# Decay rows of the mLSTM spread by one 128-row float32r product, and a 128-row low product for the last down k-tile

## The chip, the cores and the metric

One NeuronCore of one Trainium2 chip runs the whole kernel. Times are device microseconds (us) of that core, from runs of the same program; a profile is one execution seen by the hardware profiler. TensorE (PE) does the matrix products, ScalarE (ACT) and VectorE (DVE) do elementwise work, GpSimd (POOL) small side jobs, SyncE (SP) issues the transfers.

## The reference

Two layers over 256 tokens of width 1024, all in float32. Only the parts that the change touches are written out:

```python
def hybrid_layer(h, p_i, ...):
    h = h + 0.5 * swiglu(rmsnorm(h, ffn1_norm), w_gate, w_up, w_down)   # (silu(x Wg) * (x Wu)) Wd, inner width 2752
    u = rmsnorm(h, mix_norm); z = u @ w_in
    hm = mlstm_chunkwise(mq, mk, mv, ig, lf)        # 4 heads of 256
    ha = swa_gqa_sinks(aq, ak, av, a_sinks)
    h = h + (sigmoid(g_m) * (hm @ w_branch_m) + sigmoid(g_a) * (ha @ w_branch_a)) @ w_out
    h = h + 0.5 * swiglu(rmsnorm(h, ffn2_norm), ...)
    return h + sigmoid(rmsnorm(h, ple_norm) @ ple_gate_w) * (p_i @ ple_proj_w)

# inside mlstm_chunkwise: per head, weights exp(a[s] - M[t]) between tokens s <= t,
# a = input gate - running sum of log forget gates, M = running maximum of a
```

## The kernel before

Each float32 product is carried by float32r products of parts: x = xh + xl and w = wh + wl, where the high part is rounded to float32r and the low part is the rest; `mm3` issues xh·wh, xh·wl and xl·wh into one PSUM accumulation. Weights stream from memory in raw tiles of 1 MB (two buffers). Each is cut into parts of 128 x 1024; ScalarE rounds a part into `wh`, VectorE subtracts to get `wl` (`splitting`), and eight split parts fit on the chip. TensorE, ScalarE, VectorE and SyncE issue in the order in which the Python code runs; `tick()` advances background chains (generators that yield where the next stage has to wait) by an estimated clock, `Clock`, so a chain with one stage more is issued later. GpSimd's order is left to the framework.

A layer runs ffn1, mix, ffn2 and the per-layer embedding (ple). Two places matter.

The down product of an ffn (`down_run`; tile `dn`; 4 in the program) has 2752 = 21·128 + 64 inner rows, so 22 k-tiles. k-tiles 0 to 17 go to all four outputs (token tile t, half n) in turn. The last four go output by output: 3 + 3 + 3 + 2 products for one output, then the next. For the last k-tile the hidden layer's 64 rows are stored twice in one tile of 128 rows, the high part on rows 0 to 63 and the low part on 64 to 127, against the weight rows, also stored twice. One 128-row product gives xh·wh + xl·wh; the product xh·wl takes 64 rows only (`p=low`, `lo[low]`).

The decays of the mLSTM (`decays`, tile `wt`; 4 heads in each of 2 layers) need the row -M[t] of a head on all 128 partitions. The four rows lie in `nM`, 4 x 384 in float32. A float32 product of 4 rows with one column of the identity, broadcast over 128 columns, spreads one of them; two bf16 products add the causal mask. These groups stand between the products of branch A (tile `ya`), in the chain `scans`, after five small transposes of the gates (`tp<-ident,gates`) and their copy `gcols`.

The norm that follows an ffn (`norm`: sums on ACT, `ms` on DVE, the power `r` on POOL, `xn` on DVE, transposes on TensorE) begins for token tile 0 while TensorE works on the outputs of token tile 1.

Of the kernel before, what the change touches and what calls it, by code (L numbers as in the profile page):

```python
# [11 lines left out]
F32 = mybir.dt.float32  # L12
# [21 lines left out]
RAW = 2                 # raw weight tiles  # L34
RING = 8                # split weight parts on chip
STORE, HASTE = 4, 3     # parts split and not begun: enough of them, and what suffices in haste
AHEAD = (3.0, 2.0)      # how far the splitting engines' queues may be ahead of TensorE: until STORE is reached, then
ACTIVE = 5              # attention groups at work at a time
LATE = 4                # k-tiles of the hidden layer that come output by output
# [10 lines left out]
class Part:  # L50
    """k k-tiles of n weight columns, from column c0 of the raw tile: split into high and low when fed."""

    def __init__(self, c0, k, n):
        self.c0, self.k, self.n = c0, k, n
        self.hi = self.lo = self.ready = None
        self.fresh = True


class Clock:
    """An estimate (us) of when each engine is through with what it was given, from which the order of issue follows.  # L60
    The instructions of a stage take each other's results: an engine's first one starts after the others' so far, and
    VectorE's also after ScalarE's."""
# [43 lines left out]
    def load(self, ready, mb=1.0):  # L106
        """A transfer that may start at ready -> when it arrives."""
        latency, per = self.DMA
        self.dma = max(self.dma, ready, self.now) + mb * per
        return self.dma + latency  # L110


class Timed:
    """An engine whose instructions are charged to the clock."""
# [25 lines left out]
class XT:  # L140
    """The two parts of a transposed activation [nk * 128, T]: hi, lo(k, tok[, n]) is n of its k-tiles (one: 2-d).
    wait() moves the chains on that still have to write what is about to be read."""
# [20 lines left out]
class Trunk:  # L163
    """Every float32 product x @ w is carried as xh @ wh + xh @ wl + xl @ wh, where
    xh is x rounded to float32r and xl = x - xh, which float32r holds exactly.

    TensorE, ScalarE and VectorE issue in the order written here. The products with the weights are cut into steps
    of about 1.3 us; before each, tick() splits weights that come later and moves the chains in the background
    (norms, transposes, attention) on, so that what TensorE meets next has been ready for a while."""

# [24 lines left out]
    def tick(self):  # L195
        """Moves on the chains whose next stage is ready by TensorE's time, then feeds."""
        for chain in list(self.bg):
            if chain[1] <= self.clock.now:
                self.advance(chain)
        self.feed()  # L200
# [9 lines left out]
    def later(self, chain, ready=0.0):  # L210
        """A generator: it yields where what follows has to wait for what it issued."""
        self.bg.append([chain, max(self.clock.done(), ready)])
        return self.bg[-1]
# [13 lines left out]
    def defer(self, fn, *args):  # L227
        """fn(*args), once what it reads is ready; what it yields, if anything, are stages of a chain."""
        def chain():
            more = fn(*args)  # L230
            if more is not None:
                yield from more
        return self.later(chain())

# [13 lines left out]
    def consts(self):  # L248
# [9 lines left out]
        nc.vector.memset(self.ones, 1.0)  # L258

        def mask(out, base, step, channel):  # L260
            """0 where base + step * column + channel * row >= 0, else NEG."""
# [11 lines left out]
    def load(self, parts, *copies):  # L273
        """Registers a load, in the order of use: copies (raw -> destination, DRAM source) and what it is cut into."""
# [3 lines left out]
    def columns(self, src, p=None):  # L278
        """Registers src [128, k, n]."""
# [5 lines left out]
    def unit(self, w, c0, n=NB):  # L285
        """Registers columns c0..c0+n of w [1024, .]."""
# [7 lines left out]
    def halves(self, src):  # L294
        """Registers two units by halves of their k-tiles; src(u, h) is a list of (raw -> view, DRAM source)."""
# [11 lines left out]
    def prefetch(self, n=RAW, cut=False):  # L307
        """Issues loads until n raw tiles are under way (cut: each in two transfers)."""
# [12 lines left out]
    def feed(self, must=False):  # L321
        """Starts to split the next weight part if it is there and the queues are short enough, or if it must."""
# [20 lines left out]
        def chain():  # L343
            yield from self.splitting(hi, lo, raw[:, part.c0 : part.c0 + w])
# [12 lines left out]
    def need(self, part):  # L357
        """Has part split before a product with it is issued."""
# [20 lines left out]
    def project(self, units, xT, base, use, first=0, last=0):  # L379
        """x @ each unit; use(n, t, ps) takes unit n for token tile t. The first and the last parts are used for token  # L380
        tile 0 and then for token tile 1, the others for both at once."""
# [29 lines left out]
    def project_T(self, unit, xT, base):  # L411
        """(x @ unit)^T -> PSUM banks [features, 2 * T], two feature tiles in each."""
# [4 lines left out]
    def project_halves(self, units, xT, base, use):  # L417
        """The same for each unit; use(i, ps) takes the feature tiles i, i + 1. The first half of x's k-tiles goes to
        all units before the second does."""
# [36 lines left out]
    def transposes(self, src, n):  # L456
        """src [P, n*128] -> PSUM [P, n, 128]."""
# [28 lines left out]
    def first_gain(self, vec):  # L486
        """The same in PSUM: products with ones, which also have TensorE's clock up when the first rows arrive."""
# [12 lines left out]
    def power(self, out, x):  # L500
        """out = x ** -0.5"""
        self.nc.gpsimd.tensor_tensor(out, x, self.mhalf[:, : x.shape[-1]], op=ALU.pow)

    def norm(self, t, ss, g, xT):
        """A chain: the normed token tile, transposed and split into xT."""
# [15 lines left out]
    def first_norm(self, t, g, xT):  # L521
        """The norm of the input; the first weight part's split (entry) goes between its products and its copies."""
# [11 lines left out]
    def sink(self, scale, following):  # L534
        """(prepare, then): then(n, t, y) adds scale * y to half n of token tile t of the residual stream and goes on
        to the norm that follows: (gain vector, xT), or None after the last block."""
# [22 lines left out]
    def ffn(self, xT, wg, wu, wd, sink, first=6):  # L559
# [22 lines left out]
        def swiglu(pg, pu, k):  # L582
            """A chain: the transposed hidden layer from k-tile k on, from silu(gate) and banks [features, n * T]. Of the
            last rows, high and low lie one below the other in the first part's tile."""
# [23 lines left out]
        def last_features(c0):  # L608
            """The last features' gate and up columns side by side in one stationary tile."""
# [15 lines left out]
        for k0 in range(0, nk - 2, 2):  # L625
# [3 lines left out]
                          *[(lambda raw, p=p: raw[p, D:], wd[(nk - 1) * P :, :]) for p in (low, high)])  # L629

        def down_run():
# [3 lines left out]
            def tile_mm(t, n, k):  # L635
# [4 lines left out]
                else:  # L640
                    nc.tensor.matmul(acc[t, n], hT[0](k, tok), hi, start=False, stop=False)
                    nc.tensor.matmul(acc[t, n], hT[0](k, tok, p=low), lo[low], start=False, stop=True)
# [22 lines left out]
    def ple(self, l, xT, sink):  # L665
        """sigmoid(x) is (1 + tanh(x / 2)) / 2 here and in mix, as tanh shares a table with silu and with exp; the sink's
        scale takes the half in."""
# [42 lines left out]
    def mix(self, l, xT, sink):  # L710
        """ga, gm and the merged branches carry twice their values, which the sink's scale takes back."""
# [37 lines left out]
        def job_T(units, xT, base, use, before=None):  # L749
            """use(k, ps) takes the k-tiles k, k + 1 of the transposed product [features, 2 * T]."""  # L750
# [6 lines left out]
        def gate(c0):  # L757
            """tanh(gate / 2) by k-tiles, transposed."""
# [47 lines left out]
    def per_feature(self, l):  # L806
        """Per-partition columns: conv taps (k, tile), conv bias (tile), q and k gains (both halves)."""
# [60 lines left out]
class Mlstm:  # L868
    """Matrix memory in parallel form over two blocks of 128 tokens."""
# [7 lines left out]
    def prepare(self, w_in):  # L877
        """The loads for the gates."""
# [10 lines left out]
    def gate_weights(self):  # L889
        """The 8 gate columns as a stationary tile of 128: high i, f at columns 0, 32, low i, f at columns 64, 96."""  # L890
# [8 lines left out]
    def log_gates(self):  # L899
        """With F the running sum of log f inside a block of 128 tokens, a = i - F, M the running maximum of a and of  # L900
        what the block starts from, m = F + M: cols = per-token columns a0, a0 + F0[last], a1, m0, m1 (block number;
        4 heads each), em = exp(-m), nM = rows -[M0 | M1 | M1]."""
# [10 lines left out]
    def scans(self, ps):  # L913
# [26 lines left out]
        self.nM = nM  # L940
# [13 lines left out]
    def values(self, n, t, ps):  # L954
        """v split per token block: [P, heads, 258] with a column of ones after each head."""
# [10 lines left out]
    def qk_job(self, w_in, part, hp):  # L966
        """silu(causal conv(x @ w_in[q or k columns of heads 2hp, 2hp+1])), transposed and split."""
# [32 lines left out]
    def decays(self):  # L1000
        """Per head the weights exp(a - M) of [s, t] for s in block 0, t in both, and s, t in block 1."""
        tr, nc = self.tr, self.nc
        N = T + P
        for hd in range(MH):
            ps = tr.bank("wt")[:, :N]
            nc.tensor.matmul(ps, tr.ident[:MH, hd : hd + 1].to_broadcast([MH, P]), self.nM, start=True, stop=False,
# [73 lines left out]
class Swa:  # L1080
    """Sliding-window attention of 16 query heads over 4 key heads. Key head b*2+g and its 4 query heads j sit at
# [179 lines left out]
```

## Time and profile before

| | us |
|---|---|
| median of 3 runs (lowest to highest) | 1411.66 (1410.39 to 1412.22) |
| profiled execution, span | 1409.6 |
| TensorE busy | 1394.8 |
| VectorE busy | 862.7 |
| ScalarE busy | 728.0 |
| GpSimd busy | 50.1 |

The span runs from the first to the last instruction; the runs' time also holds what lies around it (2.1 us between the span and the median). Matmuls are pipelined and the profiler models their ends, so the time of one is read from the distance between starts, not from its recorded duration. PEld is the load of the stationary operand.

### The profile page before, as it was taken

To read this page: it belongs to the slowest core of one execution; us is meant where nothing else is said; L and a number is where in the kernel's file an instruction comes from. 1 tells how busy PE (TensorE), PEld (TensorE's weight loads), DVE (VectorE), ACT (ScalarE), POOL (GpSimd) and SP (SyncE) were. 2 spreads that over 40 slices of the span, in tenths; PEclk is the share of its full clock that TensorE was granted. 3 is DMA by queue.
4 is the path that set the end of the run, shared out by engine and by line. 5 is a ranking of instruction groups with operands and counts; after the bars stand their busy time and mean duration, and the time that the engine had idled before them with its cause. 6 is when DMAs were issued, how large, how long until landed. Compare 5 with 4: busy or idle time off the path is not lost.

```text
span 1409.6 us, 21951 instructions
## 1 busy us (share of the span) xinstructions
PE 1394.8 (99%) x9064; PEld 1247.4 (88%) x9064; DVE 862.7 (61%) x1209; ACT 728.0 (52%) x1136; POOL 50.1 (4%) x78
## 2 busy tenths in 40 slices
PE   8999999999999999999999999999999999999998
PEld 6999877899999889988779998778998998999876
DVE  5656457655887665454575554675658876555544
ACT  5544346765655454443554444467646654544433
POOL 0000012000000000000000000120000000000000
PEclk9999999999999999999999999999999999999999
DMA  6665645354545565565456566443545544765651
GB/s 214 220 205 174 216 138 180 109 132 151 193 151 179 165 193 196 165 232 179 164 174 206 168 209 203 147 143 104 145 150 195 172 158 162 221 193 172 204 177 60
DMA packets 125830, 243.81 MB, mean 173 GB/s; under 512 B 14977, under 2 KB 23841, under 8 KB 125730
## 3 DMA queue, kind: packets, MB, share of 16 engines
q1 hardware_dynamic: 125730, 242.41, 53.6%
q8 instruction: 71, 1.16, 0.3%
q14 instruction: 29, 0.24, 0.1%
HBM read 241.34 MB, written 1.05 MB: 172 GB/s over the span
## 4 chain that ended last, share of the span: by engine, by line
PE 95%; DMA 2%; DVE 2%; ACT 1%; issue 0%; POOL 0%; SPq 0%; ACTq 0%
PE dn L129 17%; PE pg L129 15%; PE pu L129 14%; PE gt L129 7%; PE z L129 6%; PE gu L129 6%; PE kvq L129 5%; PE ya L129 3%; PE v L129 3%; PE ym L129 3%; PE og L129 3%; PE yo L129 3%; PE tp L129 3%; PE sc L129 2%; PE ha L129 1%; DVE wl L129 1%
## 5 line engine op out<-in xcount | busy, mean ns | idle before, releaser
L129 DVE TENSOR_TENSOR wl<-raw,wh 128x1024 fp32r<-128x1024 f32 x448 | 541.4, 1222 | 371.0 <-ACT wh L129 367.8
L129 ACT CAST wh<-raw 128x1024 fp32r<-128x1024 f32 x448 | 461.9, 1049 | 422.9 <-PE dn L129 92.4
L129 PE MATMUL dn<-wh,hid 128*128 128x512 f32 x688 | 219.2, 397 | 0.0
L129 PE MATMUL pg<-uT,wh 128*128 128x256 f32 x1088 | 194.7, 281 | 0.0
L129 PE MATMUL pu<-uT,wh 128*128 128x256 f32 x1088 | 193.8, 280 | 0.0
L129 PEld LDWEIGHTS pg<-uT,wh 128*128 128x128 f32 x1088 | 167.2, 189 | 0.2
L129 PEld LDWEIGHTS pu<-uT,wh 128*128 128x128 f32 x1088 | 167.2, 189 | 0.0
L129 PEld LDWEIGHTS dn<-wh,hid 128*128 128x128 f32 x688 | 129.2, 188 | 32.4 <-issue 2.9
L129 PE MATMUL pu<-uT,wl 128*128 128x256 f32 x544 | 153.3, 282 | 0.0
L129 PE MATMUL pg<-uT,wl 128*128 128x256 f32 x544 | 153.3, 282 | 0.0
L129 PE MATMUL dn<-wl,hid 128*128 128x512 f32 x352 | 140.6, 399 | 0.0
L129 PEld LDWEIGHTS pg<-uT,wl 128*128 128x128 f32 x544 | 102.3, 188 | 0.0
L129 PEld LDWEIGHTS pu<-uT,wl 128*128 128x128 f32 x544 | 102.3, 188 | 0.0
L129 PE MATMUL gt<-uT,wh 128*128 128x256 f32 x512 | 93.7, 284 | 0.0
L129 PE MATMUL z<-uT,wh 128*128 128x256 f32 x512 | 92.3, 282 | 0.0
L129 PE MATMUL gu<-wh,uT 128*128 128x512 f32 x256 | 83.9, 404 | 1.7 <-ACT uT L129 1.7
L129 PEld LDWEIGHTS dn<-wl,hid 128*128 128x128 f32 x352 | 66.1, 188 | 19.5 <-issue 5.3
L129 PEld LDWEIGHTS gt<-uT,wh 128*128 128x128 f32 x512 | 78.9, 189 | 1.3
L129 PEld LDWEIGHTS z<-uT,wh 128*128 128x128 f32 x512 | 78.6, 188 | 0.2
L129 PE MATMUL z<-uT,wl 128*128 128x256 f32 x256 | 72.0, 281 | 0.0
L129 PE MATMUL gt<-uT,wl 128*128 128x256 f32 x256 | 71.9, 281 | 0.0
L129 PE MATMUL kvq<-wh,uT 128*128 128x512 f32 x192 | 63.4, 400 | 0.0
(188 smaller groups left out, 2057.4 us busy)
## 6 DMA issues: line engine op xcount, KB each, us to landing
raw<-in_w_in_dram SPq DMA_DIRECT2D x60, 1024.0 KB, 4.9
raw<-in_ffn_w_up_dram SPq DMA_DIRECT2D x40, 1024.0 KB, 5.0
raw<-in_ffn_w_down_dram SPq DMA_DIRECT2D x40, 1024.0 KB, 5.1
raw<-in_ffn_w_gate_dram SPq DMA_DIRECT2D x39, 1024.0 KB, 5.1
raw<-in_w_branch_a_dram SPq DMA_DIRECT2D x16, 512.0 KB, 5.8
raw<-in_w_branch_m_dram SPq DMA_DIRECT2D x8, 1024.0 KB, 4.9
raw<-in_w_out_dram SPq DMA_DIRECT2D x8, 1024.0 KB, 4.9
raw<-in_ple_gate_w_dram SPq DMA_DIRECT2D x8, 1024.0 KB, 5.9
```

Of the source, the lines that this page charges most:

```text
L129: return issue(*args, **kw)
```

## The change

Two edits (those that only take out comments and docstrings are left out). The first puts high and low parts of the four rows into a constant 128-row float32r tile of zeros, high on rows 0 to 3, low on rows 32 to 35, and spreads with a 128-row selector `pick` that has ones in both places. The second gives the last down part's `wl` zeros in rows 64 to 127 (a memset on GpSimd), lets VectorE write rows 0 to 63 only, and takes all 128 rows in the product.

```diff
+        self.pick = c.tile([P, MH], F32R, name="pick")
+        self.rows2 = c.tile([P, T + P], F32R, name="rows2")
+        for x in (self.pick, self.rows2):
+            nc.gpsimd.memset(x.bitcast(F32), 0.0)
+        for r in (slice(0, MH), slice(32, 32 + MH)):
+            nc.vector.tensor_copy(self.pick[r], self.ident[r, r])
...
         def chain():
-            yield from self.splitting(hi, lo, raw[:, part.c0 : part.c0 + w])
+            src = raw[:, part.c0 : part.c0 + w]
+            if part.rows is None:
+                yield from self.splitting(hi, lo, src)
+            else:
+                self.tc.nc.gpsimd.memset(lo[part.rows.stop :].bitcast(F32), 0.0)
+                self.nc.scalar.copy(hi, src)
+                yield
+                r = part.rows
+                self.nc.vector.tensor_tensor(lo[r], src[r], hi[r].bitcast(F32), op=ALU.subtract)
...
+        down[-1].rows = low
...
-                    nc.tensor.matmul(acc[t, n], hT[0](k, tok, p=low), lo[low], start=False, stop=True)
+                    nc.tensor.matmul(acc[t, n], hT[0](k, tok), lo, start=False, stop=True)
...
-        self.nM = nM
+        yield
+        yield from tr.splitting(tr.rows2[:MH], tr.rows2[32 : 32 + MH], nM)
...
-            nc.tensor.matmul(ps, tr.ident[:MH, hd : hd + 1].to_broadcast([MH, P]), self.nM, start=True, stop=False,
+            nc.tensor.matmul(ps, tr.pick[:, hd : hd + 1].to_broadcast([P, P]), tr.rows2, start=True, stop=False,
                              skip_group_check=True)
```

The chain `scans` has two stages more, so its instructions move back among the products of branch A. TensorE's order before, in branch A of the first layer, at the third of the four decay groups (`wl_3060` and `wh_3059` are parts of the branch's weights, `wt_3399` the head's bank):

```order
L129 MATMUL ya_3179<-qT_131,wl_3060 128x256
L129 MATMUL wt_3399<-nM_3177,ident 128x384
L129 LDWEIGHTS identb
L129 MATMUL wt_3399<-mask_st,identb 128x128
L129 LDWEIGHTS identb
L129 MATMUL wt_3399<-mask_st,identb 128x128
L129 MATMUL ya_3178<-qT_131,wh_3059 128x256
```

The same place now, where the first of the four groups stands (`rows_93` is the constant tile of rows, `wl_3067` and `wh_3066` the same weight parts as above):

```order
L130 MATMUL ya_3186<-qT_137,wl_3067 128x256
L130 MATMUL wt_3390<-rows_93,pick 128x384
L130 LDWEIGHTS identb
L130 MATMUL wt_3390<-mask_st,identb 128x128
L130 LDWEIGHTS identb
L130 MATMUL wt_3390<-mask_st,identb 128x128
L130 MATMUL ya_3185<-qT_137,wh_3066 128x256
```

The group has the same instructions as before with other operands, and all four groups of a layer stand two groups later among the same products.

VectorE's order before, in the same stage, behind the rows `nM` (`wl` are weight parts, `gcols` the transposed gates, `qT` attention outputs):

```order
L129 TENSOR_SCALAR nM_3177<-gates_3176 4x128
L129 TENSOR_TENSOR wl_3234<-raw_3097,wh_3233 128x1024
L129 TENSOR_TENSOR qT_133<-ha_3075,qT_131 128x4x128
L129 COPY gcols_3319<-tp_3304 128x20
L129 TENSOR_TENSOR wl_3296<-raw_3097,wh_3295 128x1024
L129 TENSOR_TENSOR wl_3311<-raw_3204,wh_3310 128x1024
```

VectorE's order now, at the same place:

```order
L130 TENSOR_SCALAR nM_3184<-gates_3183 4x128
L130 TENSOR_TENSOR wl_3241<-raw_3104,wh_3240 128x1024
L130 TENSOR_TENSOR qT_139<-ha_3082,qT_137 128x4x128
L130 TENSOR_TENSOR wl_3303<-raw_3104,wh_3302 128x1024
L130 TENSOR_TENSOR rows_93<-nM_3184,rows_93 4x384
L130 TENSOR_TENSOR wl_3313<-raw_3211,wh_3312 128x1024
L130 TENSOR_TENSOR wl_3338<-raw_3211,wh_3337 128x1024
L130 COPY gcols_3368<-tp_3353 128x20
```

One subtraction for the low rows is new, and the copy of the gates stands behind three weight parts where it stood ahead of them. On ScalarE a cast of the same 4 x 384 rows is new. Outside branch A no instruction of TensorE, ScalarE or SyncE changes its place.

## Rows read from the trace of the kernel before

**Rows 1.** The page: busy time by engine, and the chain that ended last.

```profile
PE 1394.8 (99%) x9064; PEld 1247.4 (88%) x9064; DVE 862.7 (61%) x1209; ACT 728.0 (52%) x1136; POOL 50.1 (4%) x78
...
PE 95%; DMA 2%; DVE 2%; ACT 1%; issue 0%; POOL 0%; SPq 0%; ACTq 0%
```

**Rows 2.** Waits of PEld: total us, times, longest.

```profile
PEld dn L129 <- issue: 8.2, 28, 0.4
PEld L129 <- issue: 7.6, 20, 0.5
PEld sc L129 <- issue: 4.5, 20, 0.2
```

**Rows 3.** Groups by shape, PEld: busy us, mean ns, idle before.

```profile
L129 PEld LDWEIGHTS dn<-wl,hid 128*128 128x128 f32 x336 | 63.2, 188 | 14.2
...
L129 PEld LDWEIGHTS dn<-wl,hid 64*128 64x128 f32 x16 | 2.9, 183 | 5.3 <-issue 5.3
```

**Rows 4.** Timeline of PE in the first down product: start, us, tile.

```profile
186.53 0.39 PE L129 MATMUL dn<-wl,hid 128*128 128x512 f32 x1
...
189.30 0.40 PE L129 MATMUL dn<-wl,hid 128*128 128x512 f32 x1
...
190.09 0.50 PE L129 MATMUL dn<-wl,hid 64*128 64x512 f32 x1
...
193.04 0.50 PE L129 MATMUL dn<-wl,hid 64*128 64x512 f32 x1
```

**Rows 5.** Timeline of PE at the end of the second down product.

```profile
678.14 0.50 PE L129 MATMUL dn<-wl,hid 64*128 64x512 f32 x1
...
678.91 0.39 PE L129 MATMUL pp<-wl,pT 128*128 128x512 f32 x1
```

**Rows 6.** Timeline of PE in branch A of the first layer.

```profile
327.31 0.91 PE L129 MATMUL wt<-nM,ident 4*128 4x384 f32 x2
328.14 0.28 PE L129 MATMUL wt<-mask_st,identb 128*128 128x128 bf16 x2
...
328.56 0.28 PE L129 MATMUL ya<-qT,wl 128*128 128x256 f32 x1
...
328.92 0.28 PE L129 MATMUL ya<-qT,wl 128*128 128x256 f32 x1
...
329.98 0.28 PE L129 MATMUL ya<-qT,wl 128*128 128x256 f32 x1
...
330.55 0.91 PE L129 MATMUL wt<-nM,ident 4*128 4x384 f32 x2
```

**Rows 7.** Busy time of the engines in branch A, first layer.

```profile
300.00:346.00 46.00, 46.00 (x359) 42.52 (x358) 27.67 (x43) 25.90 (x46) 0.00 (x0) 1.00 0.46 139
```

**Rows 8.** Instructions that read the decay weights `w`: ns min/median/max, first and last start.

```profile
L129 DVE SCALAR_TENSOR_TENSOR ws<-st,w x8: 550/556/559, 379.6 to 1133.5; 128x384 f32<-128x384 f32 x8
```

**Rows 9.** Groups by shape, POOL.

```profile
L1099 POOL MEMSET vpad<- 128x1024 f32 x4 | 3.7, 953 | 0.0
```

**Rows 10.** Timeline around the end of the first down product, idle before in brackets.

```profile
177.82 1.22 DVE L129 TENSOR_TENSOR wl<-raw,wh 128x1024 fp32r<-128x1024 f32 x1 [1.58 <-ACT wh L129]
...
195.30 0.55 POOL L129 TENSOR_TENSOR r<-ms,mhalf 128x1 f32<-128x1 f32 x1 [181.35 <-DVE ms L129]
195.88 1.42 DVE L129 SCALAR_TENSOR_TENSOR xn<-h,r,g 128x512 f32<-128x512 f32 x2 [0.66 <-POOL r L129]
...
198.63 1.03 PE L129 MATMUL tp<-ident,xn 128*128 128x128 f32 x8
...
204.52 1.41 DVE L129 SCALAR_TENSOR_TENSOR xn<-h,r,g 128x512 f32<-128x512 f32 x2 [0.44 <-POOL r L129]
...
206.66 1.04 PE L129 MATMUL tp<-ident,xn 128*128 128x128 f32 x8
```

**Rows 11.** Timeline at the start of the program.

```profile
5.55 0.16 DVE L129 SCALAR_TENSOR_TENSOR ms<-ss 128x1 f32<-128x1 f32 x1 [3.52 <-ACT sq L129]
```

More of the change, by code (lines that the diff above doesn't have):

```diff
@@ L56, in __init__ @@
         self.fresh = True
+        self.rows = None
 class Clock:
```

## The prediction

> **What bounds the kernel now.** I read the page first: TensorE is busy 99% of the span and holds 95% of the chain that ended last, the other engines 61% and less [rows 1]. So what counts is what the change does to TensorE's own stream; work on other engines costs only where TensorE comes to wait for it. Busy is not the same as working, so I went to the waits of the weight loads next. In mid-kernel TensorE waits for hardly any engine, but its loads stand idle with no cause that the profile can name ("issue"): 28 times in the down products, 20 times before a load of the bf16 identity, 20 times in the attention scores [rows 2]. The groups by shape say which: a load of 64 rows in the down product has 5.3 us of such idle time over 16 instances, while 336 loads of 128 rows from the same weights have none put down to it [rows 3]. The scores, with the same sign, are the other place where 64-row products stand among 128-row ones. So a change in the number of rows, from 128 to fewer or back, makes the next load wait instead of running beside the product ahead of it. The count fits: 3 outputs in each of 4 down products have a wait on the way in and one on the way out (24), and the last output of each adds one (28). Both edits take such changes of shape out of TensorE's stream.
>
> **The down products.** Undisturbed, 12 products of 128 rows and 512 columns go from 186.53 to 189.30, which is 0.231 us each [rows 4]. From one 64-row product to the next, 190.09 to 193.04, is 2.95 us for 11 products (3 + 3 + 3 + 2). Eleven at 0.231 are 2.54, so an output pays 0.41 for its 64-row product. This holds for 12 outputs: 4.9 us. At the last output of a down product the next stage follows directly: from the 64-row product at 678.14 to the second product of the next stage at 678.91 is 0.77 where two take 0.46 [rows 5], 0.31 behind it; what is lost ahead of it is hidden in the transposes there, so I take 0.31 for these four: 1.2 us. Saved: 6.1 us. Afterwards the product has the shape of its neighbours, and I give it their 0.231. Ends: 4.9, if the four last outputs gain nothing, and the 8.2 us that all loads of the down products idle [rows 2].
>
> **The decay groups.** From one group to the next, 327.31 to 330.55, is 3.24 us, with 18 products of branch A between [rows 6]. Nine of those take 328.92 to 329.98, or 0.118 each, so 18 take 2.12 and the group 1.12. Its spreading product appears as two records in the trace and holds TensorE from 327.31 to 328.14, 0.83 us; the two masks and two branch products take 328.14 to 328.56, 0.42, of which 0.18 is the masks'. The new spreading product, 128 rows and 384 columns of float32r, is in no row. The nearest are 0.118 for 256 columns and 0.231 for 512, so I take 0.17, midway. The new group costs 0.35, the saving is 0.77, and with 8 groups 6.2 us. The lower end: the new product costs as much as one of the old one's two records (0.42), and its load still waits 0.2, half of what a change of shape costs above; then the group is 0.18 + 0.42 + 0.2 = 0.80 and 8 groups save 2.6. The upper end: the masks, of 128 columns each, go at half of the 0.118 for 256, 0.12 for both instead of 0.18, and the groups save 8 x 0.83 = 6.6.
>
> The trace has two records for one float32 product, and the group would lose 0.83 − 0.17 = 0.66 by this product alone, the rest by the load ahead of it. The Trainium skill ("FP8 and Floating Point Precision", TensorE Precision Notes) says that true float32 takes four passes through the array; a quarter of 0.83 left over would save 0.62 in each of 8 groups, 5.0 instead of 6.2, as an estimate, and 1400.5 as a time. The trace shows two records rather than four, so I stay with the distances between starts.
>
> **What is added, and what hides it.** In each layer a cast on ScalarE and a subtraction on VectorE of 4 x 384; the nearest row is VectorE's 128 x 384 at 0.56 [rows 8], so about 1.1 us a layer if nothing covered it. In this stage VectorE is busy 27.67 and ScalarE 25.90 of 46 us while TensorE is never idle [rows 7]: cost 0. The gate copy now waits behind three weight parts, and ScalarE's exponentials behind it; the groups move back by two, some 6.5 us (2 x 3.24). The first that reads the weights `w` is at 379.6 [rows 8], against a last group that ended at 338.2 (327.31 + 3 x 3.24 + 1.12) and now ends about 344.7. Cover about 35 us.
>
> The memset of 64 x 1024 on GpSimd costs about 0.95 (a 128 x 1024 one [rows 9]) four times. TensorE now waits for GpSimd as well as VectorE before the first product that reads this part. VectorE ends that part at 179.04, and TensorE takes it at 190.09 [rows 4, 10], a cover of 11 us; GpSimd has nothing to do for 181 us before the norm's power at 195.30. What is queued behind the memset is that power, about 16 us later. Cost 0. VectorE's subtraction of 64 rows instead of 128 has the same number of columns; I count no change. The constants at the start (two memsets, two small copies) lie ahead of `ms`, for which VectorE idles 3.52 us [rows 11]: 0.
>
> **What comes late next.** TensorE reaches the norm's transposes earlier. For token tile 0 `xn` is done at 197.30 and TensorE wants it at 198.63; for token tile 1 at 205.93 and 206.66 [rows 10]. Between the output that starts the chain and the transposes TensorE gains about 0.41 + 0.2 for tile 0 and 0.31 for tile 1. Covers of 1.33 and 0.73 shrink to about 0.7 and 0.4: no wait. The rest of the stages is only shifted.
>
> **Sum.** 6.1 + 6.2 = 12.3 us off a span of 1409.6, so 1397.3. The runs' median stands 2.1 us above this span, so the time is 1411.66 − 12.3 = 1399.4 us.
>
> **Rivals.**
>
> *The number of rows is not the cause.* The 0.41 belongs to the place (the last k-tile ends an accumulation, another output follows) and stays; only the decay groups gain: 1411.66 − 6.2 = 1405.5. For it: every 64-row product stands at that place. Against it: the scores show idle loads with 64 rows elsewhere. The Trainium skill ("TensorE: Matmul & The Clock Gate", Why this matters for your kernels) says that a product with 32 rows takes the same time as one with 128; by that rule 64 rows cost what 128 do and the second edit is worth nothing. Rows 3 and 4 speak against applying it to a product among others of another shape.
>
> *Given back downstream.* The norm's chain, a few tenths longer than I count, or the weight parts behind it, take 0.4 to 1.5 us back in each of the four transitions: 12.3 − 1.6 to 6 gives 1401.0 to 1405.4. For it: covers of only 0.73. Against it: the chain's own start moves earlier too.
>
> *The new spreading product is dear*, by the lower end above: 1411.66 − 6.1 − 2.6 = 1403.0. No row excludes it, since no row has a selector of one column broadcast over 128 with 128 rows.
>
> *Slower: GpSimd comes late.* One mechanism: the memset waits until its buffer is free, behind earlier work in GpSimd's queue, and TensorE stands at the first output's 128-row low product until it is done. It must be over 11 us late to be felt, and about 14 us late in each of the four down products to cost the 12.3 us back. At 15 us late (4 us each, 16 in all) the time is 1415.4. Against it: GpSimd's 181 idle us.
>
> **How the numbers follow.** Forecast 0.80, rows not the cause 0.04, given back 0.07, dear product 0.07, GpSimd late 0.02. A measurement of this kernel can tell about 0.2%, 2.8 us, from no change; the first four are all beyond it, so faster has 0.97, and 0.01 is left for gains that cancel, 0.02 for slower. The range takes the ends of the unknown costs: 8.2 + 6.6 = 14.8 saved is 1396.9, and 4.9 + 2.6 = 7.5 saved is 1404.2.
>
> **What would show it.** Right: no tile of 64 or 4 rows under `dn` and `wt`; no "issue" wait under `dn`; starts of 2.54 us per output in the last four k-tiles; 8 records of the spreading product, not 16, and 2.47 us (2.12 + 0.35) from group to group; the transposes of `xn` with no new wait. Wrong: an output that still takes 2.95 (the place is the cause), a group of 0.8 or more, a wait of `dn` for POOL, or weight parts that TensorE waits for behind the norm.

## The result and the profile after

| | before | after |
|---|---|---|
| median, us (lowest to highest, runs) | 1411.94 (1410.39 to 1415.15, 6) | 1403.28 (1401.18 to 1407.82, 6) |
| profiled execution, span | 1409.6 | 1400.0 |

The ratio is 0.9936 (95% interval 0.9916 to 0.9955): 0.64% faster. Forecast were 1399.4 and a range to 1404.2, so the time lies in the range, 3.9 us above the forecast: 8.7 us saved instead of 12.3.

The page of the kernel after, busy time by engine and chain, answers to [rows 1]:

```profile
PE 1384.3 (99%) x9056; PEld 1249.0 (89%) x9056; DVE 863.0 (62%) x1213; ACT 727.8 (52%) x1138; POOL 53.8 (4%) x84
...
PE 93%; DMA 3%; DVE 2%; ACT 1%; issue 1%; POOL 0%; SPq 0%; ACTq 0%; POOLq 0%
```

TensorE has 8 records fewer. Its share of the chain fell from 95% to 93%; DMA rose from 2% to 3%, a first hint that a transfer now stands in the way somewhere. The waits of the weight loads after (total us, times, longest):

```profile
PEld tp L130 <- DVE xn L130: 6.0, 2, 3.1
PEld sc L130 <- issue: 4.5, 20, 0.2
...
PEld L130 <- issue: 3.3, 12, 0.3
```

Of [rows 2] the wait under `dn` (28 times, 8.2 us) is gone. Of the 20 ahead of a bf16 identity 12 are left: the 8 of the decay groups went. The scores, which the change leaves alone, have the same 4.5. The groups by shape hold no load of 64 rows under `dn` any more [rows 3]: the 16 joined the 336.

```profile
L130 PEld LDWEIGHTS dn<-wl,hid 128*128 128x128 f32 x352 | 66.2, 188 | 15.1
```

TensorE's timeline at the end of the first down product, the first product of each of three outputs:

```profile
190.10 0.40 PE L130 MATMUL dn<-wh,hid 128*128 128x512 f32 x1
...
192.64 0.40 PE L130 MATMUL dn<-wh,hid 128*128 128x512 f32 x1
...
195.17 0.40 PE L130 MATMUL dn<-wh,hid 128*128 128x512 f32 x1
```

An output takes 2.54 and 2.53 us where it took 2.95 [rows 4]. The end of the second down product [rows 5] reads

```profile
672.52 0.39 PE L130 MATMUL dn<-wl,hid 128*128 128x512 f32 x1
...
672.98 0.39 PE L130 MATMUL pp<-wl,pT 128*128 128x512 f32 x1
```

0.46 instead of 0.77. In branch A, two decay groups [rows 6]:

```profile
329.92 0.33 PE L130 MATMUL wt<-rows,pick 128*128 128x384 f32 x1
330.09 0.28 PE L130 MATMUL wt<-mask_st,identb 128*128 128x128 bf16 x2
330.19 0.48 PE L130 MATMUL ya<-qT,wh 128*128 128x256 f32 x2
...
332.40 0.33 PE L130 MATMUL wt<-rows,pick 128*128 128x384 f32 x1
```

One record for the spreading product, 0.17 to the next start, 0.10 from the first mask to the next branch product, which then takes 0.20 instead of 0.12; 2.48 from group to group, so the group takes 0.36 beside the 2.12 of the branch's products.

The starts of the same product in both profiles, subtracted, show where the gain came and where some of it went (my alignment of the two traces; minus is earlier after):

| place | shift ahead, us | shift behind | gained |
|---|---|---|---|
| down product, layer 1, first | -0.12 | -1.51 | 1.39 |
| decays, layer 1 | -1.56 | -4.58 | 3.02 |
| down product, layer 1, second | -4.35 | -5.94 | 1.59 |
| end of the embedding block, layer 1 | -5.94 | -3.60 | -2.34 |
| down product, layer 2, first | -3.60 | -4.91 | 1.31 |
| decays, layer 2 | -4.90 | -7.92 | 3.02 |
| down product, layer 2, second | -8.10 | -9.68 | 1.58 |

The edited places gain 5.9 and 6.0, together 11.9 of the 12.3 forecast. 2.3 us are given back at one place that nobody edited. There the timeline after (all engines; in brackets the idle time before and what ended it) is

```profile
677.36 1.42 DVE L130 SCALAR_TENSOR_TENSOR xn<-h,r,g 128x512 f32<-128x512 f32 x2 [0.44 <-POOL r L130]
678.69 1.22 DVE L130 TENSOR_TENSOR wl<-raw,wh 128x1024 fp32r<-128x1024 f32 x1
678.80 0.34 SPq L498 DMA_DIRECT2D g<-in_ffn_norm_dram  x1
679.02 1.04 PE L130 MATMUL tp<-ident,xn 128*128 128x128 f32 x8
679.94 0.37 SPq L324 DMA_DIRECT2D raw<-in_ple_gate_w_dram  x1
...
686.64 2.00 ACT L130 CAST wh<-raw 128x1024 fp32r<-128x1024 f32 x2 [4.96 <-DMA raw<-in_ple_gate_w_dram]
...
690.97 1.05 ACT L130 CAST wh<-raw 128x1024 fp32r<-128x1024 f32 x1 [2.33 <-DMA raw<-in_ffn_w_gate_dram]
...
702.79 1.82 PE L130 MATMUL tp<-ident,xn 128*128 128x128 f32 x8 [2.48 <-DVE xn L130]
```

and the same rows before:

```profile
682.62 1.41 DVE L129 SCALAR_TENSOR_TENSOR xn<-h,r,g 128x512 f32<-128x512 f32 x2 [0.44 <-POOL r L129]
683.95 1.22 DVE L129 TENSOR_TENSOR wl<-raw,wh 128x1024 fp32r<-128x1024 f32 x1
684.06 0.34 SPq L483 DMA_DIRECT2D g<-in_ffn_norm_dram  x1
684.96 1.04 PE L129 MATMUL tp<-ident,xn 128*128 128x128 f32 x8
685.19 0.37 SPq L317 DMA_DIRECT2D raw<-in_ple_gate_w_dram  x1
...
691.20 2.00 ACT L129 CAST wh<-raw 128x1024 fp32r<-128x1024 f32 x2 [3.59 <-DMA raw<-in_ple_gate_w_dram]
...
706.91 1.32 PE L129 MATMUL tp<-ident,xn 128*128 128x128 f32 x8 [0.66 <-DVE xn L129]
```

`xn` of the second token tile is the last reader of the old gain, and SyncE issues the new gain `g` 0.02 us after it ends. The next weight transfer, behind `g` in SyncE's queue, waits for something else: for the raw buffer that it fills, which the subtraction `wl` behind `xn` in VectorE's order still reads. That one ends at 679.91 (678.69 + 1.22), and the transfer goes out 0.03 later; before it ends at 685.17, and the transfer follows after 0.02. So the transfer is tied to `xn` by VectorE's order. The chain to that `xn` (sums, squares, power, each on another engine) moved less than TensorE, 5.26 us against 5.94: the transfer is issued 0.23 us after TensorE's transposes before, 0.92 after. ScalarE's casts wait for it in order, its later sums behind them, and TensorE meets the norm at the end of the block 2.48 late instead of 0.66. The clock then follows. A stretch behind that wait (us, busy time of PE, PEld, DVE, ACT and POOL, granted clock, DMA share, GB/s):

```profile
702.80:706.50 3.70, 3.70 (x14) 3.17 (x15) 1.98 (x3) 2.47 (x5) 0.00 (x0) 0.54 0.02 4
```

0.54 is almost all 1.2 GHz, where the 2.80 us ahead of it, in which TensorE mostly stood, still had 2.4. So 1.8 of the 2.3 us are the longer wait and about 0.5 the lower clock.

### The profile page after: what moved, and what is told of

The parts are those of the page before. It is cut to its first block, busy times and chain, and to the rows that moved or that the text cites. A ratio compares the mean times of both kernels' runs of the same rounds, so it can differ in the third digit from the quotient of the medians.

```text
span 1400.0 us, 21954 instructions
## 1 busy us (share of the span) xinstructions
PE 1384.3 (99%) x9056; PEld 1249.0 (89%) x9056; DVE 863.0 (62%) x1213; ACT 727.8 (52%) x1138; POOL 53.8 (4%) x84
## 4 chain that ended last, share of the span: by engine, by line
PE 93%; DMA 3%; DVE 2%; ACT 1%; issue 1%; POOL 0%; SPq 0%; ACTq 0%; POOLq 0%
PE dn L130 16%; PE pg L130 15%; PE pu L130 14%; PE gt L130 7%; PE z L130 7%; PE gu L130 6%; PE kvq L130 5%; PE ya L130 3%; PE v L130 3%; PE ym L130 3%; PE og L130 3%; PE yo L130 3%; PE tp L130 3%; PE sc L130 2%; DMA raw<-in_ffn_w_gate_dram 1%; PE ha L130 1%
## 5 line engine op out<-in xcount | busy, mean ns | idle before, releaser
L130 DVE TENSOR_TENSOR wl<-raw,wh 128x1024 fp32r<-128x1024 f32 (+1 forms) x448 | 541.5, 1222 | 372.8 <-ACT wh L130 369.3
```

The costliest lines, as they stand in the source:

```text
L130: return issue(*args, **kw)
```

## The experiments

Runs of one kernel differ by some us here because TensorE falls to 1.2 GHz for some 10 us in part of them (last section), so beside medians I give the median of the runs whose mean granted clock was 0.998 or more (called full clock). It is 1410.6 for the kernel before (10 such of the 22 runs of one batch, median 1414.08) and 1401.5 for the kernel after (5 of 12), 9.1 apart.

**The down edit alone.** The kernel after with the decays as before:

```diff
-            nc.tensor.matmul(ps, tr.pick[:, hd : hd + 1].to_broadcast([P, P]), tr.rows2, start=True, stop=False,
+            nc.tensor.matmul(ps, tr.ident[:MH, hd : hd + 1].to_broadcast([MH, P]), self.nM, start=True, stop=False,
```

> Only the second edit (the last down part's low product with 128 rows and zeros); the decays are as before. Theory A (a change in the number of rows makes the next weight load wait): four last k-tiles of an output take 2.54 us instead of 2.95, no issue wait under dn, 6.1 us saved in TensorE's stream, about 1405.8 us where the kernel before takes 1411.9. Rival B (the 0.41 us belongs to the place): outputs still take 2.95, no gain, 1411.9. Rival C (about 2.3 us are given back at the end of the first embedding block whenever TensorE arrives there earlier): 6.1 saved, 2.3 lost, 1408.1, with a wait for xn there of about 2.5 us instead of 0.7.

Measured: 1410.01 (11 runs), ratio 0.9953 (0.9935 to 0.9971); at full clock 1405.2, that is 5.4 below before. Its down products gain 1.3 to 1.6 each, as in the whole change. The transfer above is issued 0.63 after the transposes, and TensorE waits 1.44. So the second edit is worth about what was forecast, and it alone brings 0.40 of the 0.69 by which the transfer is later.

**The decay edit alone.** The kernel after without the zero rows:

```diff
-        down[-1].rows = low
...
-                    nc.tensor.matmul(acc[t, n], hT[0](k, tok), lo, start=False, stop=True)
+                    nc.tensor.matmul(acc[t, n], hT[0](k, tok, p=low), lo[low], start=False, stop=True)
```

> Only the first edit (decay rows by one 128-row float32r product); the down products are as before. Theory A: groups 2.47 us apart plus moved work, 8 records of the spreading product, 6.2 us saved in TensorE's stream, about 1405.7 us where the kernel before takes 1411.9; together with the down edit alone the savings add up to the 12.3 us of both. Rival C (2.3 us given back at the end of the first embedding block): 1408.0, with a wait for xn of about 2.5 us there. If the wait is chance, of the DMA and not of the change, it may or may not stand in this profile.

Measured: 1410.40 (12 runs), ratio 0.9974 (0.9954 to 0.9994); the one run at full clock took 1403.7. Each decay stage gains 3.0. At full clock that is 6.9 below before; 5.4 and 6.9 add up to the 12.3 that the expectation names, but both edits together gave 9.1. The 6.9 rests on one run, and how much of the 3.2 between is the wait for `xn` stays open. The profiled execution, with the span at 1413.6, looks slower than before; its windows tell why:

```profile
238.30:248.50 10.20, 10.20 (x30) 7.28 (x29) 5.26 (x13) 7.73 (x29) 1.56 (x1) 0.50 0.00 0
709.30:712.70 3.40, 3.40 (x13) 2.68 (x11) 1.56 (x3) 2.60 (x4) 0.00 (x0) 0.51 0.02 5
938.00:948.20 10.20, 10.20 (x29) 7.22 (x29) 5.79 (x15) 7.73 (x29) 1.91 (x9) 0.50 0.00 0
```

Three stretches at 1.2 GHz; the aligned starts lose 4.5 us at each long one. None of them is at a place that the edit touches. Nor is the wait for `xn` at the end of the embedding block, ahead of the middle one:

```profile
708.87 0.55 PE L130 MATMUL tp<-ident,xn 128*128 128x128 f32 x3 [2.41 <-DVE xn L130]
```

The transfer is issued 0.25 after the transposes, as before, but takes 7.60 to its first cast, and 2.3 us are lost there by the aligned starts. So a wait as long as that of the whole change comes without any later issue.

**Place or shape.** The kernel before with the 64-row k-tile ahead of the last full one:

```diff
-                    for k in range(late, nk):
+                    for k in (*range(late, nk - 2), nk - 1, nk - 2):
```

> The kernel before, with the last k-tile's two products (one of 64 rows) issued ahead of the last full k-tile, so that the 64-row product no longer ends an accumulation and no output follows it. Theory A: the 0.4 us stays with the 64-row product at its new place (wait of its load, and of the load behind it, 0.24 to 0.36 us each), and the outputs are 2.95 us apart as before; time about that of the kernel before, 1411.9. Rival B (the end of an accumulation costs it): no extra time around the 64-row product, outputs 2.54 us apart, about 6 us less.

Measured: 1417.63 (1 run, one stretch at 1.2 GHz in it). Its timeline around two 64-row products, which no longer end an accumulation:

```profile
190.24 0.50 PE L130 MATMUL dn<-wl,hid 64*128 64x512 f32 x1
190.67 0.50 PE L130 MATMUL dn<-wh,hid 128*128 128x512 f32 x1
191.00 0.40 PE L130 MATMUL dn<-wl,hid 128*128 128x512 f32 x1
...
193.19 0.50 PE L130 MATMUL dn<-wl,hid 64*128 64x512 f32 x1
```

2.95 from one to the next, as before: the price goes with the shape. 0.43 and 0.33 to the next two starts, where 0.23 is usual, are 0.3 of it.

**Shape or type in the decays.** The spreading product with 128 rows, zeros in 124 of them, but in float32; the down edit is left out:

```diff
-        self.rows2 = c.tile([P, T + P], F32R, name="rows2")
+        self.rows2 = c.tile([P, T + P], F32, name="rows2")
...
-        yield from tr.splitting(tr.rows2[:MH], tr.rows2[32 : 32 + MH], nM)
```

> The kernel before, with the decay rows still one float32 product but of 128 rows, zeros in the other 124 (selector and rows kept in zeroed 128-row tiles, no split). It tells the part of a group's saving that belongs to the shape from the part that belongs to the type. Theory A (both): the two records of the product stay, about 0.32 us each for 384 columns, the load ahead of them no longer waits; a group costs 0.9 to 1.0 us instead of 1.12, so 1 to 2 us in all. Rival (the type alone): a group costs 1.12 as before. Rival (the shape alone): it costs 0.35 to 0.4.

Measured: 1407.53 (1 run at full clock). A decay stage gains 1.2, or 0.3 a group. The instructions of `wt` in it (ns min/median/max, first and last start):

```profile
L130 PE MATMUL wt<-rows,pick x16: 483/486/487, 326.8 to 1030.0; 128*128 128x384 f32 x16
```

Two records for each product again. So of the 0.76 a group, 0.3 is the number of rows and some 0.45 the type. The group costs 0.81, under the 0.9 to 1.0 expected. At the same 128 rows the float32 product holds TensorE for 0.64 us, 3.7 times the 0.17 of float32r, where the records alone would say twice.

**Does a later cast mend the wait?** The kernel after with transfers planned 2.5 us later in the order of work:

```diff
-    DMA = (1.0, 2.9)
+    DMA = (3.5, 2.9)
```

> The changed kernel with the planner's estimate of a transfer's latency raised from 1.0 to 3.5 us, so that ScalarE's casts of weight parts are issued later and stand less often, waiting for a transfer, ahead of the activations that the norm needs. Theory D: the wait for xn at the end of the first embedding block shrinks to under 1 us, about 2 us less than the changed kernel in undisturbed runs (1399.5). Rival: the wait is bound by the norm's own chain, or the later casts make TensorE wait for weight parts elsewhere; same time or slower.

Measured: 1470.28 (4 runs), ratio 1.0398 (1.0372 to 1.0423). TensorE's waits:

```profile
PE gu L130 <- DVE wl L130: 12.2, 10, 3.1
PE pu L130 <- ACT wh L130: 4.2, 3, 1.4
```

The transposes at the end of the first embedding block wait for nothing here, but the weight parts come late all over the kernel, TensorE with them, and so this is no test. The rival won; the way to start this one transfer earlier was not found.

**Chance or the change?** The two kernels unchanged, three more profiles of each (the first of the kernel after also timed: 1406.21, ratio 0.9928, 0.9902 to 0.9954).

> The changed kernel once more. Its profile had a wait of 2.48 us for xn at the end of the first embedding block (0.66 before) and 3.4 us of half granted clock behind it, together 2.3 us of the 12.3 given back there, after one weight transfer whose last packets came late. Theory D (chance: a late transfer that ScalarE's queue stands on): a new profile has the wait at another size or not at all, and the fastest runs are near 1399.5 to 1401. Rival C (structural): the wait is about 2.5 us again and no run is under 1401.

> The kernel before, for a second profile. Theory D (the wait for xn at the end of the first embedding block is chance of the transfers): it is not 0.7 us again but between 0.7 and 2.5, as in the kernel with the decays alone, which changes nothing near this place and had 2.4. Rival C (the change brings it): 0.7 again, no granted-clock fall there.

> The changed kernel a third time, for one number: how long TensorE waits for the normed rows of the first token tile at the end of the first layer's embedding stage (2.5 and 2.1 us in its two profiles so far, 0.7 and 1.3 in the two of the kernel before). Theory (chance of the transfers): the wait lies anywhere from 0.3 to 2.6 us, as it does over the partial kernels, and the four new profiles of the two kernels overlap. Rival (the shortened stream brings it): here 2.0 us or more again, with TensorE at half clock for some 3.4 us behind it.

> The kernel before a third time, for the same wait. Theory (chance of the transfers): anywhere from 0.3 to 2.6 us. Rival (the shortened stream brings the wait): 1.5 us or less, as in both profiles so far.

> The changed kernel a fourth time, for the same wait. Theory (chance of the transfers): anywhere from 0.3 to 2.6 us, so that with the third one at least one of two should fall under 2.0. Rival (the shortened stream brings it): 2.0 us or more.

> The kernel before a fourth time, for the same wait. Theory (chance of the transfers): anywhere from 0.3 to 2.6 us, so that with the third one at least one of two should rise over 1.5. Rival (the shortened stream brings it): 1.5 us or less.

The last four took 1409.39 and 1406.17 (after), 1416.67 and 1414.53 (before), one run each; the second profile of before 1414.89. At the end of the first embedding block, by profile:

| | before (4 profiles) | after (4 profiles) |
|---|---|---|
| transposes to issue of the transfer, us | 0.23, 0.24, 0.25, 0.23 | 0.92, 0.91, 0.91, 0.92 |
| issue to the first cast of it | 6.01, 6.74, 7.34, 6.42 | 6.70, 6.83, 6.77, 7.19 |
| TensorE's wait for `xn` | 0.66, 1.25, 1.96, 0.95 | 2.48, 2.12, 2.04, 2.48 |

The longest wait before, in its third profile:

```profile
683.80 1.04 PE L129 MATMUL tp<-ident,xn 128*128 128x128 f32 x8
684.05 0.37 SPq L317 DMA_DIRECT2D raw<-in_ple_gate_w_dram  x1
...
707.06 1.84 PE L129 MATMUL tp<-ident,xn 128*128 128x128 f32 x8 [1.96 <-DVE xn L129]
```

Neither expectation held whole. Chance is there: the transfer takes 6.0 to 7.3 us to its cast, and the wait before follows it in order. Issue and transfer together, less the wait, are 5.6 to 5.7 in seven of the eight profiles (5.1 in the first of after, where ScalarE waits another 2.33 for the transfer behind it), so the wait is what these two leave uncovered. Kernels that leave this place alone show the spread too: 2.41 with the decays alone (7.60 from issue to cast), 0.26 in the run of the float32 product (5.61). That the four waits of each kernel don't overlap is therefore no proof by itself. But one row has no chance in it: the issue is 0.68 later in every profile after. The change brings 0.7 us; the mean waits, 1.21 and 2.28, differ by 1.07, and of the rest 0.24 is the transfers of these eight profiles. The first profile of before, from which I predicted, holds the shortest wait of the four. TensorE falls to 1.2 GHz for 3.4 us behind the wait in two of the four profiles after (2.48 both) and in one before (1.96), not behind 2.04 and 2.12.

The 0.68 has two parts. With the down edit alone the issue stands 0.63 after the transposes, 0.39 later than the mean before. The other 0.29 goes with GpSimd's power for the first token tile, at the start of this norm:

```profile
668.43 0.16 DVE L130 SCALAR_TENSOR_TENSOR ms<-ss 128x1 f32<-128x1 f32 x1 [0.79 <-ACT sq L130]
...
669.09 0.55 POOL L130 TENSOR_TENSOR r<-ms,mhalf 128x1 f32<-128x1 f32 x1 [17.57 <-DVE ms L130]
```

It starts 0.50 us behind the end of `ms`, in all four profiles after (0.49 to 0.50), against 0.14 in the four before and 0.15 with the down edit alone. The padded scores below, which hold the whole change, have 0.15 too, and the issue at 0.66. GpSimd has been idle for 17.57 us by then; why it starts late, no row says.

**The third place with 64 rows.** The kernel after with each key head's keys in 128 rows, zeros where the other head's lie, so that the score products take 128 rows too:

```diff
-                    nc.tensor.matmul(ps[:, j, :], self.qT[x](4 * p + j0 + j, tok, p=rows), self.kT[rows, y, p, :S],
+                    nc.tensor.matmul(ps[:, j, :], self.qT[x](4 * p + j0 + j, tok), self.kT[g][:, y, p, :S],
```

> The changed kernel, with the last 64-row products made 128-row ones too: the keys of each half of a pair of key heads lie in a tile of their own with zeros in the other 64 rows, so that the score products take all 128 rows. Theory A (changes of shape): each of the 24 score groups loses its waits, some 0.35 us, 7 to 8 us in all; undisturbed runs near 1393 to 1394 where the changed kernel has 1401.4. Theory E (the granted clock falls to half for 10 us behind the first score groups in about half of the executions because of their 64-row products): no such fall, and the runs lie within 2 to 3 us of each other instead of 9. Rival (the falls come from the waits around attention, not from the row count): falls stay, a spread of 6 us or more.

Measured: 1393.66 (1392.14 to 1394.25, 5 runs), ratio to before 0.9851 (0.9829 to 0.9873): faster than both kernels. Two score groups that follow each other, in its timeline:

```profile
233.92 0.39 PE L130 MATMUL sc<-band,identb 128*128 128x512 bf16 x1
233.96 1.64 PE L130 MATMUL sc<-kT,qT 128*128 128x128 f32 x12
235.44 0.39 PE L130 MATMUL sc<-band,identb 128*128 128x512 bf16 x1
```

and in the second profile of the kernel after:

```profile
233.30 0.39 PE L130 MATMUL sc<-band,identb 128*128 128x512 bf16 x1
233.62 1.55 PE L130 MATMUL sc<-kT,qT 64*128 64x128 f32 x12
235.10 0.39 PE L130 MATMUL sc<-band,identb 128*128 128x512 bf16 x1
```

1.52 instead of 1.80 for a group, though twice the rows are multiplied. Inside a group the products start 0.11 us apart in both, with 64 rows and with 128: the price is paid at its two ends. Of the 24 groups 8 are of this shape; the other 16, of six products with 256 columns, go from 1.22 to 0.93 where two follow each other. That makes about 7 us of the 7.9 between the full-clock medians, 1401.5 and 1393.7. The mean clock was 0.998 or more in all five runs.

## Why the prediction was right, and where it was off

*The bound and the cause.* Right. TensorE's stream set the time, and in the down products the number of rows was the cause: the wait under `dn` went, the price stayed with the 64-row product when that was moved, and the rival "rows not the cause" (1405.5) falls. In the decay groups the rows are 0.3 of 0.76 and the type the rest. By the Trainium skill ("TensorEngine Tiling (Array Packing)", Key Properties) a change of tiling mode drains TensorE; the trace agrees that a change of rows costs something, with 0.41 us an output here; no run shows the drain itself. Equal times for few and many rows, which I had weighed as a rival, are found between products inside a score group (0.11 us each way), but not for a product among others of another shape.

*The down products.* 5.9 us against 6.1. The output period is 2.54, as forecast; the last outputs of the two products that go on to the mixer's `kvq` gain about 0.2 less each than the other two.

*The decay groups.* 6.0 against 6.2: 3.02 a layer, 0.36 a group against 0.35. The spreading product takes 0.17, the value chosen between two rows; the dear product (0.42 and a wait) falls. The masks cost the 0.18 that I had kept: 0.10 to the next start, and 0.08 more on the branch product behind them, as before the change. The upper end, 0.12 for both, was not reached. (The time that I gave for the four passes should be 1400.6, not 1400.5.)

*What is added.* Right at nothing where I looked for it; GpSimd's power that starts 0.36 later in one place (above) I did not foresee. GpSimd's memset is done long before its product, ahead even of VectorE's half:

```profile
176.47 0.95 POOL L355 MEMSET wl<- 64x1024 f32 x1 [162.59 <-PE dn L130]
...
177.71 1.22 DVE L130 TENSOR_TENSOR wl<-raw,wh 64x1024 fp32r<-64x1024 f32 x1 [1.57 <-ACT wh L130]
```

so "GpSimd late" falls, and the weights `w` come in time for their first reader at 375.0.

*What comes late next.* Here a step failed: "Covers of 1.33 and 0.73 shrink to about 0.7 and 0.4: no wait. The rest of the stages is only shifted." The covers did shrink, to 0.6 and 0.6 in the first down product, with no wait there. But at the second down product of layer 1 the cover of `xn` for the second token tile shrank from 0.93 to 0.24, by 0.69 and not 0.31, and I followed the norm to TensorE only: behind `xn` VectorE has a subtraction to do that frees the buffer of the next weight transfer. That lead was used up, and the block behind it started 2.3 us later in the profile than it could. This is the rival "given back downstream" at one of its four places, with a little more than the 1.5 us it allowed; of the 2.3 about 0.7 are the later issue, which every profile shows, and the rest is the transfer's spread and the clock, which other profiles have at other sizes.

*The sum.* 12.3 forecast; 0.4 less in the sized terms and 2.3 given back leave the 9.6 between the two spans. From there to 8.7 between the medians is the spread of runs with and without a stretch at 1.2 GHz; at full clock the kernels are 9.1 apart. That the median lies in the range is in part luck: three of its six runs took 1401 to 1402, the other three, at a lower mean clock, 1405 to 1408, and six later runs of the same kernel have a median of 1406.21, above the range (with before at 1414.08).

## What to carry to other kernels

Where TensorE is the bound and its loads idle with no cause named, group them by shape: a few products with fewer rows among full ones cost more than the multiplications that they save, and zeros in the free rows are the cheaper way, if another engine has time to write them. When a shorter stretch on the bounding engine moves a norm's chain, follow what stands behind the chain's last step on its own engine too: here a subtraction whose end frees the buffer of the next transfer. One profile holds one draw of each transfer; a lead of less than a microsecond is read from several.

## What the runs showed of the hardware

In 12 of 22 runs of the kernel before, and in 7 of the 9 of a later batch, the mean granted clock was under 0.998, and the profiles show why: behind the first score groups, in either layer or both, TensorE goes from 2.4 to 1.2 GHz for some 10 us while it is busy throughout. In the second profile of the kernel after:

```profile
225.00:237.00 12.00, 12.00 (x68) 9.72 (x66) 8.68 (x14) 5.41 (x7) 4.05 (x3) 1.00 0.71 238
237.40:247.60 10.20, 10.20 (x30) 7.19 (x29) 5.63 (x15) 7.73 (x29) 1.91 (x9) 0.50 0.00 0
248.00:260.00 12.00, 12.00 (x65) 9.18 (x65) 8.19 (x19) 7.33 (x21) 0.00 (x0) 1.00 0.36 102
```

It costs 4.5 to 4.6 us each time by the aligned starts. Ahead of the fall stand two score groups of twelve 64-row products each, and with those products at 128 rows the profile has no such fall behind its scores, nor has any of the five runs by its mean clock:

```profile
225.00:237.00 12.00, 12.00 (x71) 10.15 (x69) 9.47 (x16) 6.13 (x9) 4.50 (x3) 1.00 0.71 242
237.00:248.00 11.00, 11.00 (x66) 9.23 (x65) 8.00 (x24) 8.14 (x30) 2.84 (x9) 1.00 0.03 9
```

That points to the 64-row products as what lets the clock fall; five runs without a fall, where 7 of the 9 runs of the kernel before in the same batch have the lower clock, are not a proof, and why only some executions fall stays open.
